# The low part of a weight tile: a negated copy on ACT and an adding DMA, instead of a subtraction on POOL

## The chip, the core and the metric

The program runs on one core of a Trainium2 chip. The metric is the time of one execution on the device in microseconds (us), as the median of several runs. The engines are TensorE (PE in the profile, its weight loads PEld), VectorE (DVE), ScalarE (ACT), GpSimd (POOL) and SyncE (SP, which here only issues DMAs).

## What is computed

Two layers of a decoder trunk over 512 tokens of width 1024, all in float32. Each layer projects the normalised input to the queries, keys and values of two kinds of attention and to gates; the results are merged, projected, normalised and added to the input; then comes a feed-forward block with a squared ReLU. Cut to the products, which are what the weights are loaded for:

```python
for layer in range(2):
    proj = rms_norm(x, g[0]) @ w_in            # 1024 -> 4504: q, k, v of both attentions, gates
    kc, vc = compress(k_c, w1[0]), compress(v_c, w1[1])   # blocks of 32 keys, MLP 2048 -> 256 -> 64
    y_nsa = sparse_attention(q, kc, vc, k_s, v_s, k_w, v_w, gates) @ w_nsa_o
    y_sb = stick_breaking_attention(sb_q, sb_k, sb_v) @ w_sb_o
    mixed = (sigmoid(g_a) * y_nsa + sigmoid(g_b) * y_sb) @ w_out
    x = x + rms_norm(mixed, g[1])
    ff = square(relu(rms_norm(x, g[2]) @ w_ff1)) @ w_ff2  # 1024 -> 4096 -> 1024
    x = x + rms_norm(ff, g[3])
```

## The kernel before

TensorE multiplies in a rounded float32 format (F32R). To keep float32's accuracy every operand is split in two: a high part, the value rounded, and a low part, the value minus the high part. A product of a weight w and an activation a is three matmuls into one bank of PSUM: w.hi x a.hi, w.hi x a.lo and w.lo x a.hi (`three`, L168 to L172).

Weights come in tiles of 128 x 1024 (512 KB), each with the weights of one output tile: 8 blocks of 128 x 128, so 24 matmuls over 512 tokens. A tile of the compression's `w1` feeds only 8 matmuls over 256 columns. `Weight` makes a tile ready in three steps, each on another engine. SP's queue loads it into `w_raw`, of which there are two buffers. ACT copies it, rounded, into `w_hi` (L146). POOL subtracts, raw minus high, into `w_lo` (L147). Three buffers each of `w_hi` and `w_lo` go round: a tile's copy can start when TensorE has finished with the tile three before. A few tiles of the compression have `sub=V`: there VectorE subtracts. Tiles whose tag isn't "w" (the first of a product after a norm) are made in two halves, on the same engines (L153, L154).

The order of TensorE's instructions is that of the program, written out by hand with a table of numbers (`PLAN`) that says how many matmuls of a projection stand between two steps of the attention. The orders of the other engines and of the DMA queues are made by a scheduler as the program is built. Every engine takes its instructions in order: what waits holds up all behind it.

A layer has these stages in the trace (layer 0, then layer 1 some 810 us later): the projections beside the sparse attention (to about 330 us, its first half up to about 165 us with the compression and the rotary embedding on VectorE), the merge and `w_out`, the norm and residual in `tail` (about 430 to 490 us), the feed-forward (to about 780 us), and another `tail`.

Of the kernel before, what the change touches and what calls it, by code (L numbers as in the profile page):

```python
# [8 lines left out]
F32 = mybir.dt.float32  # L9
F32R = mybir.dt.float32r  # L10
I32 = mybir.dt.int32
AF = mybir.ActivationFunctionType
ALU = mybir.AluOpType
# [12 lines left out]
P = 128  # L26
# [23 lines left out]
def layer_kernel(ctx, tc, xT, pos, gvec, tri, consts, smalls, w_in, w1, w_o, w_out, ff1, ff2, out):  # L50
    nc = tc.nc
    V, S, G, E = nc.vector, nc.scalar, nc.gpsimd, nc.tensor

    cp = ctx.enter_context(tc.tile_pool(name="cp", bufs=1))
    sp = ctx.enter_context(tc.tile_pool(name="sp", bufs=1))
# [6 lines left out]
    def big(tag, name, dt=F32):  # L62
        return sp.tile([P, T], dt, tag=tag, bufs=BUFS[tag], name=name)
# [4 lines left out]
    def psum(tag, name):  # L68
        return pp.tile([P, T], F32, tag=tag, bufs=2, name=name)
# [64 lines left out]
    class Weight:  # L134
        def __init__(self, src, tag="w", sub=None, between=None):
            raw = sp.tile([P, 1024], F32, tag="wr", bufs=2, name="w_raw")
            if between is None:
                nc.sync.dma_start(raw, src)
            else:
                nc.sync.dma_start(raw[:, 0:512], src[:, 0:512])  # L140
                between()
                nc.sync.dma_start(raw[:, 512:], src[:, 512:])
            if tag == "w":
                h = sp.tile([P, 1024], F32R, tag="wh", bufs=3, name="w_hi")
                l = sp.tile([P, 1024], F32R, tag="wl", bufs=3, name="w_lo")
                S.activation(h, raw, AF.Copy)  # L146
                (sub or G).tensor_tensor(l, raw, h.bitcast(F32), ALU.subtract)  # L147
                self.h, self.l = [h[:, 0:512], h[:, 512:]], [l[:, 0:512], l[:, 512:]]
            else:
                self.h = [big(tag, "w_hi", F32R) for _ in range(2)]  # L150
                self.l = [big(tag, "w_lo", F32R) for _ in range(2)]
                for j in range(2):
                    S.activation(self.h[j], raw[:, 512 * j:512 * j + 512], AF.Copy)  # L153
                    (sub or G).tensor_tensor(self.l[j], raw[:, 512 * j:512 * j + 512], self.h[j].bitcast(F32), ALU.subtract)  # L154
# [13 lines left out]
    def three(ps, w, k, act, first, last):  # L168
        ah, al = act
        E.matmul(ps, w.hi(k), ah, start=first, stop=False)  # L170
        E.matmul(ps, w.hi(k), al, start=False, stop=False)  # L171
        return E.matmul(ps, w.lo(k), ah, start=False, stop=last)  # L172
# [52 lines left out]
        return [(big("act", f"ah{k}", F32R), big("act", f"al{k}", F32R)) for k in range(KT)]  # L225

    def tail(l, n, mixed, acc, load, acts, prev, src, nxt, head):
        """The last output tiles of a product, its post-norm, the residual and the next pre-norm with the first tiles of
        the product that follows, in two halves of the tokens."""
        group = range(KT - GN, KT)  # L230
        last_sq = []
        na = new_acts() if nxt is not None else None
# [172 lines left out]
            return vc  # L405

    class Filler:
        """Products emitted one at a time between the steps of the attention; `late` holds what follows a product by some
        steps."""

        def __init__(self):
            self.gens, self.late, self.n = [], [], 0
# [27 lines left out]
                    self.late.pop(0)[1]()  # L440

    class Head:
        """The first four units of a product, their weights prepared ahead of it."""

        def __init__(self, src):
            self.src, self.ws = src, []
# [10 lines left out]
    def layer(l, acts, R, heads):  # L457
# [174 lines left out]
        groups = [(g, qt, b) for g in range(2) for qt in QORD[g] for b in range(2)]  # L632
        items, first, last, late_c = [], [], [], []
# [44 lines left out]
        score = [0, 0]  # L678

        def score_ahead(i, budget):  # L680
            """Scores of the groups whose items come soon after item i, a few heads at a time."""
            while score[0] < len(groups):
                j, h = score
                if first[j] > i + 1:
                    held = sum(need(k) for k in range(j) if last[k] > i)
                    if budget <= 0 or first[j] > i + PLAN["AH"] or held + need(j) > BUFS["P"]:
                        return
                nsa_scores(j, h)
                budget -= 1
                score[:] = [j, h + 1] if h < 3 else [j + 1, 0]  # L690
# [86 lines left out]
        def turn(i):  # L777
            j, kt = items[i]
            if kt == "c":
                fill.until(lambda: groups[j][0] in softmaxed)  # L780
            nsa_turn(items[i])
            score_ahead(i, PLAN["BU"])
# [29 lines left out]
        for h in range(4):  # L812
            score_ahead(0, 1)
            fill.run(PLAN["F2"])
# [84 lines left out]
        early = {}  # L899

        def mix_in(m, j, tag, last):
            """The first terms of output tile m's product with the attention j's output."""
            if m not in early:
                early[m] = Weight(w_o[l, m]), {}
            wo, banks = early[m]
            ps = psum(tag, "y")
            src = (o_nsa, o_sb)[j]
            banks[j] = ps, last
            for k in range(last):
                three(ps, wo, 4 * j + k, src[k], k == 0, k == 3)  # L910
                yield
# [87 lines left out]
        last = l + 1 == DEPTH  # L999
# [101 lines left out]
```

## Time and profile before

| | |
|---|---|
| median of 3 runs | 1643.62 us (1638.53 to 1645.77) |
| the profiled execution, from its first to its last instruction | 1643.4 us |
| TensorE (PE) busy | 1542.5 us, 94% |
| VectorE (DVE) busy | 911.0 us, 55% |
| POOL busy | 797.8 us, 49% |
| ACT busy | 725.5 us, 44% |
| DMA: share of 16 engines' time, on SP's queue | 27.1% |
| mean granted clock of TensorE | 0.972 |

The shares are means over the stages named above, in which different engines are busy. A busy TensorE isn't TensorE at its peak, since its matmuls are pipelined: in the feed-forward one 128x512 matmul begins every 0.23 us and is recorded as 0.389 us long.

### The profile page before, as it was taken

How to read it: one execution, taken by the hardware profiler on the slowest of the kernel's cores; microseconds unless marked ns; L12 is line 12 of the kernel's file. 1: busy time of each engine (PE TensorE's matmuls, PEld its weight loads, DVE VectorE, ACT ScalarE, POOL GpSimd, SP SyncE). 2: the span in 40 equal slices, each digit the busy share in tenths (PEclk: the TensorE clock that was granted, in tenths of full speed). 3: DMA queues.
4: the chain of work that ended last, by engine and by line, in shares of the span. 5: the costliest groups of instructions: out<-in, count | busy, mean ns of one | idle time of the engine just before them, and what ended most of it. 6: DMA issues, size and time to landing. Idle time of an engine off the chain costs nothing.

```text
span 1643.4 us, 20414 instructions
## 1 busy us (share of the span) xinstructions
PE 1542.5 (94%) x7706; PEld 1291.3 (79%) x7706; DVE 911.0 (55%) x1536; ACT 725.5 (44%) x1343; POOL 797.8 (49%) x519
## 2 busy tenths in 40 slices
PE   7688999999989999999987989999998999999996
PEld 5576778888878888887885767788878888888886
DVE  8998964355493232314599888533536823223246
ACT  6355764553453232324344567655433523233242
POOL 3674444435544444445557734444455344444443
PEclk9889999999999999999998999999999999999998
DMA  5221112223423233333322210122244132332321
GB/s 180 77 79 63 29 50 77 65 82 114 138 65 103 90 103 92 101 95 110 123 78 77 90 39 26 53 77 77 90 128 128 40 102 93 100 99 94 102 91 64
DMA packets 46002, 143.14 MB, mean 87 GB/s; under 512 B 5008, under 2 KB 11536, under 8 KB 45904
## 3 DMA queue, kind: packets, MB, share of 16 engines
q1 hardware_dynamic: 45680, 141.55, 27.1%
q8 instruction: 60, 0.98, 0.3%
q14 instruction: 38, 0.31, 0.1%
q0 software_dynamic: 80, 0.26, 0.0%
q10 hardware_dynamic: 144, 0.03, 0.0%
HBM read 137.11 MB, written 4.72 MB: 86 GB/s over the span
## 4 chain that ended last, share of the span: by engine, by line
PE 74%; DVE 19%; ACT 3%; issue 2%; DMA 1%; POOL 1%; SPq 0%; DVEq 0%; ACTq 0%; POOLq 0%
PE ff L170 12%; PE ff L171 12%; PE ff L172 12%; PE proj L469 5%; PE proj L467 5%; PE proj L465 5%; DVE pn L276 2%; DVE P L675 2%; PE y L171 2%; PE p_t L705 2%; PE y L170 2%; PE y L172 2%; PE tail L171 1%; PE tail L170 1%; PE tail L172 1%
## 5 line engine op out<-in xcount | busy, mean ns | idle before, releaser
L147 POOL TENSOR_TENSOR w_lo<-w_raw,w_hi 128x1024 fp32r<-128x1024 f32 x226 | 550.9, 2439 | 569.4 <-ACT w_hi L146 558.2
L146 ACT ACTIVATE w_hi<-w_raw 128x1024 fp32r<-128x1024 f32 x230 | 243.4, 1059 | 564.2 <-PE ff L171 391.1
L467 PE MATMUL proj<-al,w_hi 128*128 128x512 f32 x496 | 199.6, 402 | 0.0
L469 PE MATMUL proj<-ah,w_lo 128*128 128x512 f32 x496 | 199.6, 402 | 0.0
L465 PE MATMUL proj<-ah,w_hi 128*128 128x512 f32 x496 | 198.5, 400 | 0.0
L171 PE MATMUL ff<-hl,w_hi 128*128 128x512 f32 x448 | 174.4, 389 | 1.2 <-DVE hl L166 1.2
L170 PE MATMUL ff<-ah,w_hi 128*128 128x512 f32 x448 | 174.3, 389 | 0.0
L171 PE MATMUL ff<-al,w_hi 128*128 128x512 f32 x448 | 174.3, 389 | 0.0
L170 PE MATMUL ff<-hh,w_hi 128*128 128x512 f32 x448 | 174.3, 389 | 0.0
L172 PE MATMUL ff<-hh,w_lo 128*128 128x512 f32 x448 | 174.3, 389 | 0.0
L172 PE MATMUL ff<-ah,w_lo 128*128 128x512 f32 x448 | 174.3, 389 | 0.0
L166 DVE TENSOR_TENSOR hl<-relu,hh 128x512 fp32r<-128x512 f32 x64 | 108.2, 1696 | 80.1 <-ACT hh L165 79.9
L996 DVE TENSOR_TENSOR ffa<-ff,ffa 128x512 f32<-128x512 f32 x40 | 27.6, 691 | 155.9 <-PE ff L172 155.9
L467 PEld LDWEIGHTS proj<-al,w_hi 128*128 128x128 f32 x496 | 95.8, 193 | 17.2
L465 PEld LDWEIGHTS proj<-ah,w_hi 128*128 128x128 f32 x496 | 95.5, 193 | 17.0
L469 PEld LDWEIGHTS proj<-ah,w_lo 128*128 128x128 f32 x496 | 95.3, 192 | 17.1 <-POOL w_lo L147 0.3
L171 PEld LDWEIGHTS ff<-hl,w_hi 128*128 128x128 f32 x448 | 84.1, 188 | 19.1 <-DVE hl L166 1.6
L172 PEld LDWEIGHTS ff<-ah,w_lo 128*128 128x128 f32 x448 | 84.1, 188 | 17.6
L172 PEld LDWEIGHTS ff<-hh,w_lo 128*128 128x128 f32 x448 | 84.1, 188 | 17.6
L171 PEld LDWEIGHTS ff<-al,w_hi 128*128 128x128 f32 x448 | 84.1, 188 | 17.5
L170 PEld LDWEIGHTS ff<-hh,w_hi 128*128 128x128 f32 x448 | 84.1, 188 | 17.3
L170 PEld LDWEIGHTS ff<-ah,w_hi 128*128 128x128 f32 x448 | 84.1, 188 | 17.2
(308 smaller groups left out, 3353.6 us busy)
## 6 DMA issues: line engine op xcount, KB each, us to landing
w_raw<-in_ff_dram SPq DMA_DIRECT2D x128, 512.0 KB, 3.5
w_raw<-in_w_in_dram SPq DMA_DIRECT2D x69, 512.0 KB, 3.5
w_raw<-in_w_dram SPq DMA_DIRECT2D x16, 512.0 KB, 3.5
w_raw<-in_w_o_dram SPq DMA_DIRECT2D x16, 512.0 KB, 3.4
w_raw<-in_w_out_dram SPq DMA_DIRECT2D x16, 512.0 KB, 3.5
x<-in_xT_dram SPq DMA_DIRECT2D x8, 256.0 KB, 6.8
x_old<-in_xT_dram SPq DMA_DIRECT2D x8, 256.0 KB, 2.7
xsave<-x SPq DMA_DIRECT2D x8, 256.0 KB, 2.0
```

The costliest lines, as they stand in the source:

```text
L146: S.activation(h, raw, AF.Copy)
L147: (sub or G).tensor_tensor(l, raw, h.bitcast(F32), ALU.subtract)
L166: V.tensor_tensor(lo, src, hi.bitcast(F32), ALU.subtract)
L170: E.matmul(ps, w.hi(k), ah, start=first, stop=False)
L171: E.matmul(ps, w.hi(k), al, start=False, stop=False)
L172: return E.matmul(ps, w.lo(k), ah, start=False, stop=last)
L276: V.scalar_tensor_tensor(t, mixed[k][:, c], gcol(l, n, k), R[:, c], ALU.mult, ALU.mult)
L465: E.matmul(ps, w.hi(k), ah, start=(k == 0), stop=False)
L467: E.matmul(ps, w.hi(k), al, start=False, stop=False)
L469: E.matmul(ps, w.lo(k), ah, start=False, stop=(k == KT - 1))
L675: V.tensor_scalar(pr[h], pr[h], sm4[:, h:h + 1], None, ALU.mult)
L705: E.transpose(pt[:, P * h:P * h + P], pend[j][0][h][:, P * kt:P * kt + P], ident)
```

## The change

For a tile with tag "w" and no `sub`, POOL's subtraction goes away. ACT writes a second copy of the raw tile, with the factor -1 and rounded as the first, into `w_lo`: minus the high part. Then a DMA, issued by POOL, reads the tile again from memory and adds it to what stands in `w_lo`: the weight minus its high part, as before. So a second read of 512 KB a tile comes, and the high part is no longer an operand of the low part's making. `w_hi` and `w_lo` have four buffers instead of three; the room for them comes from the space in which descriptors of POOL's DMAs are kept, 4,096 bytes a partition instead of the usual. Tiles with another tag, and those with `sub`, are as they were. The diff also empties some comments, so that lines behind L147 move down by 4.

```diff
             if tag == "w":
-                h = sp.tile([P, 1024], F32R, tag="wh", bufs=3, name="w_hi")
-                l = sp.tile([P, 1024], F32R, tag="wl", bufs=3, name="w_lo")
+                h = sp.tile([P, 1024], F32R, tag="wh", bufs=4, name="w_hi")
+                l = sp.tile([P, 1024], F32R, tag="wl", bufs=4, name="w_lo")
                 S.activation(h, raw, AF.Copy)
-                (sub or G).tensor_tensor(l, raw, h.bitcast(F32), ALU.subtract)
+                if sub is None:
+                    S.activation(l, raw, AF.Copy, scale=-1.0)
+                    nc.gpsimd.dma_start(l, src, accum_op=ALU.add)
+                else:
+                    sub.tensor_tensor(l, raw, h.bitcast(F32), ALU.subtract)
...
-    nc = bacc.Bacc("TRN2", target_bir_lowering=False, num_devices=1)
+    nc = bacc.Bacc("TRN2", target_bir_lowering=False, num_devices=1, dynamic_dma_scratch_size=4096)
```

The scheduler's orders change with it. The first place is ACT at the start, where the first weights of tag "w" are made beside the first norm (`R_104`, from `ss`, the sum of squares) and the tables of the rotary embedding (`nround`, `s_342`, from `ang`). Before:

```order
L146 ACTIVATE w_hi<-w_raw 128x1024
L202 ACT_TABLE_LOAD
L202 ACTIVATE R_104<-ss,eps_c 128x256
L146 ACTIVATE w_hi<-w_raw 128x1024
L202 ACTIVATE R_104<-ss,eps_c 128x256
L204 ACT_TABLE_LOAD
L204 ACTIVATE R_104<-R_104 128x256 x2
L116 ACT_TABLE_LOAD
L116 ACTIVATE nround<-ang 128x512
```

And now:

```order
L146 ACTIVATE w_hi<-w_raw 128x1024
L148 ACTIVATE w_lo<-w_raw 128x1024
L146 ACTIVATE w_hi<-w_raw 128x1024
L148 ACTIVATE w_lo<-w_raw 128x1024
L206 ACT_TABLE_LOAD
L206 ACTIVATE R_104<-ss,eps_c 128x256 x2
L116 ACT_TABLE_LOAD
L116 ACTIVATE nround<-ang 128x512
L117 ACTIVATE s_343<-ang 128x512
L129 ACT_TABLE_LOAD
L208 ACTIVATE R_104<-R_104 128x256 x2
```

The third and the fourth tile of tag "w" now stand ahead of the norm's logarithm, the first of them was between its two halves; and the norm's exponential (L204 before, L208 now) has moved behind the sines.

The second place is POOL in the sparse attention of layer 0, where it scales probabilities (`P`) between weights of `w_in` and of the compression (`w`). Before:

```order
L673 TENSOR_TENSOR P<-P,sm_624 128x512 x2
L147 TENSOR_TENSOR w_lo<-w_raw,w_hi 128x1024 x2
L132 TENSOR_TENSOR sb0l<-sbf,sb0h 128x512
L673 TENSOR_TENSOR P<-P,sm_732 128x512 x2
L147 TENSOR_TENSOR w_lo<-w_raw,w_hi 128x1024 x2
```

And now:

```order
L677 TENSOR_TENSOR P<-P,sm_629 128x512 x2
L149 DMA w_lo<-in_w_in_dram 128x1024
L149 DMA w_lo<-in_w_dram 128x1024
L677 TENSOR_TENSOR P<-P,sm_740 128x512 x2
L132 TENSOR_TENSOR sb0l<-sbf,sb0h 128x512
L149 DMA w_lo<-in_w_dram 128x1024
L149 DMA w_lo<-in_w_in_dram 128x1024
```

The DMAs' issues stand where the subtractions stood, and the second scaling has moved ahead of `sb0l`.

## Rows read from the trace of the kernel before

**Rows 1.** The page's first part, without the weight loads: busy time, share of the span and number of instructions of each engine.

```profile
PE 1542.5 (94%) x7706; PEld 1291.3 (79%) x7706; DVE 911.0 (55%) x1536; ACT 725.5 (44%) x1343; POOL 797.8 (49%) x519
```

**Rows 2.** The page's chain of the work that ended last, by engine (shares of the span).

```profile
PE 74%; DVE 19%; ACT 3%; issue 2%; DMA 1%; POOL 1%; SPq 0%; DVEq 0%; ACTq 0%; POOLq 0%
```

**Rows 3.** Busy time of each engine in four stretches, in us, with the number of its instructions; then the granted clock of TensorE (1.00 is 2.4 GHz), the busy share of the DMA engines and what they moved.

```profile
20.00:165.00 145.00, 116.85 (x565) 92.78 (x563) 133.58 (x248) 77.01 (x162) 87.24 (x57) 0.89 0.25 77
...
410.00:493.00 83.00, 75.05 (x497) 69.54 (x496) 55.43 (x90) 40.73 (x80) 43.95 (x31) 0.96 0.32 102
493.00:739.00 246.00, 246.00 (x1087) 203.71 (x1086) 72.42 (x70) 74.22 (x92) 108.11 (x45) 1.00 0.31 97
...
862.00:987.00 125.00, 103.98 (x531) 83.99 (x531) 114.34 (x248) 69.96 (x165) 76.12 (x53) 0.90 0.21 68
```

**Rows 4.** The page's costliest groups, the two that make a tile's parts: operation, operands, count, then busy us and mean ns of one, then the engine's idle time before them and what ended it.

```profile
L147 POOL TENSOR_TENSOR w_lo<-w_raw,w_hi 128x1024 fp32r<-128x1024 f32 x226 | 550.9, 2439 | 569.4 <-ACT w_hi L146 558.2
L146 ACT ACTIVATE w_hi<-w_raw 128x1024 fp32r<-128x1024 f32 x230 | 243.4, 1059 | 564.2 <-PE ff L171 391.1
```

**Rows 5.** The timeline of layer 0 around 94 us, rows of POOL, VectorE and TensorE: start and duration in us (x2 are two instructions in a row), and in brackets the idle time before and who ended it.

```profile
94.58 5.13 POOL L147 TENSOR_TENSOR w_lo<-w_raw,w_hi 128x1024 fp32r<-128x1024 f32 x2
...
94.70 2.79 DVE L336 TENSOR_TENSOR xr<-qr,xr 64x512 fp32r<-64x512 f32 x1
...
96.99 0.33 PE L365 MATMUL cmp_h<-w_lo,bhl 128*64 128x256 f32 x1 [0.62 <-POOL w_lo L147]
...
98.14 1.66 DVE L382 TENSOR_TENSOR cmp_u<-cmp_u,cmp_ht 128x64 f32<-128x64 f32 x1
99.83 0.69 DVE L336 TENSOR_TENSOR xr<-qr,xr 64x512 fp32r<-64x512 f32 x1
```

**Rows 6.** Groups of VectorE's instructions from 20 to 165 us, shapes kept apart; the number before the last bar is the mean duration of one in ns.

```profile
L336 DVE TENSOR_TENSOR xr<-qr,xr 64x512 fp32r<-64x512 f32 x8 | 7.8, 972 | 1.1 <-ACT xr L335 0.8
L330 DVE TENSOR_TENSOR qr<-qr,rope_sh 128x512 f32<-128x512 f32 x3 | 7.1, 2383 | 0.0
...
L114 DVE SCALAR_TENSOR_TENSOR ang<-nround,ang 128x512 f32<-128x512 f32 x6 | 6.2, 1027 | 0.1
...
L522 DVE TENSOR_TENSOR K2w<-kr,K1w 64x512 fp32r<-64x512 f32 x2 | 4.2, 2105 | 0.0
...
L329 DVE TENSOR_TENSOR rope_sh<-rope_sh,sinT 128x512 f32<-128x512 f32 x4 | 3.8, 960 | 0.0
```

**Rows 7.** The same lines over the whole span, least, median and longest duration in ns.

```profile
L336 DVE TENSOR_TENSOR xr<-qr,xr x16: 684/688/2831, 65.3 to 908.7; 64x512 fp32r<-64x512 f32 x16
...
L330 DVE TENSOR_TENSOR qr<-qr,rope_sh x6: 670/2197/2901, 59.5 to 890.3; 128x512 f32<-128x512 f32 x6
...
L114 DVE SCALAR_TENSOR_TENSOR ang<-nround,ang x6: 676/682/2753, 26.5 to 36.5; 128x512 f32<-128x512 f32 x6
...
L522 DVE TENSOR_TENSOR K2w<-kr,K1w x4: 687/1186/2527, 68.9 to 881.4; 64x512 fp32r<-64x512 f32 x4
...
L329 DVE TENSOR_TENSOR rope_sh<-rope_sh,sinT x8: 669/712/1752, 52.0 to 887.7; 128x512 f32<-128x512 f32 x8
```

**Rows 8.** The groups of VectorE's instructions, as in group 6, from 862 to 987 us (layer 1).

```profile
L336 DVE TENSOR_TENSOR xr<-qr,xr 64x512 fp32r<-64x512 f32 x8 | 11.7, 1465 | 0.2
...
L330 DVE TENSOR_TENSOR qr<-qr,rope_sh 128x512 f32<-128x512 f32 x3 | 5.1, 1706 | 0.0
L329 DVE TENSOR_TENSOR rope_sh<-rope_sh,sinT 128x512 f32<-128x512 f32 x4 | 4.5, 1121 | 0.0
```

**Rows 9.** Busy time in two stretches of the instructions that write or read w_lo alone, columns as in group 3 without ACT.

```profile
20.00:165.00 145.00, 43.63 (x114) 21.62 (x113) 3.41 (x2) 42.88 (x18) 0.89 0.25 77
...
862.00:987.00 125.00, 35.50 (x93) 17.72 (x93) 3.39 (x2) 35.23 (x14) 0.90 0.21 68
```

**Rows 10.** Two rows of ACT's timeline in the feed-forward (start and duration in us): the copies of two tiles that follow each other.

```profile
565.27 1.06 ACT L146 ACTIVATE w_hi<-w_raw 128x1024 fp32r<-128x1024 f32 x1 [3.19 <-PE ff L171]
...
570.71 1.06 ACT L146 ACTIVATE w_hi<-w_raw 128x1024 fp32r<-128x1024 f32 x1 [3.19 <-PE ff L171]
```

**Rows 11.** The timeline at the start, rows of ACT and one of VectorE: start and duration in us.

```profile
26.26 1.04 ACT L146 ACTIVATE w_hi<-w_raw 128x1024 fp32r<-128x1024 f32 x1
27.32 1.28 ACT L202 ACT_TABLE_LOAD   x1
28.61 0.47 ACT L202 ACTIVATE R<-ss,eps_c 128x256 f32<-128x256 f32 x1
...
38.93 0.69 DVE L501 TENSOR_TENSOR kk<-head,R 128x512 f32<-128x512 f32 x1
```

**Rows 12.** DMA issues: first the one that POOL issues, in its timeline (start, duration of the issue), then the views of issues by line, with count, KB each and median us from issue to landing.

```profile
11.75 0.70 POOL L105 DMA_DIRECT2D pos_i<-in_pos_dram  x1
...
w_raw<-in_ff_dram SPq DMA_DIRECT2D x128, 512.0 KB, 3.5
...
pos_i<-in_pos_dram POOLq DMA_DIRECT2D x1, 256.0 KB, 6.1
```

## The prediction, made before the changed kernel was run

> **What bounds the kernel now.** I read the shares of the page first [rows 1]: TensorE is busy 94% of the span, POOL 49%, ACT 44%. A half-busy POOL proves nothing either way, so the chain that ended last comes next [rows 2]: TensorE 74%, VectorE 19%, POOL only 1%. The work that the change takes away is hardly ever the last thing waited for. The stretches say where [rows 3]: from 493 to 739 us (feed-forward) TensorE is busy without a gap, and its clock is granted at 1.00 (2.4 GHz). From 20 to 165 us and from 862 to 987 us (first half of the attention, one stretch a layer) VectorE is busy 133.6 of 145 us and 114.3 of 125 us, TensorE far less, with 0.89 and 0.90 of the clock. So there are two regimes: feed-forward, where preparing weights must only keep up, and the attention's start, where VectorE is late.
>
> **What the removed subtraction costs today.** There are 226 of them, 2,439 ns each, 550.9 us of POOL [rows 4]. In the feed-forward none is on the path. At the attention's start they are, through VectorE: the reader should lay the rows at 94 us side by side [rows 5]. POOL starts two subtractions at 94.58; VectorE's xr, begun at 94.70, takes 2.79 us, and the next xr, at 99.83, 0.69 us. In between, a 128x64 product takes 1.66 us, until POOL's second subtraction is done. A VectorE instruction with two operands in SBUF waits for the POOL subtraction to end.
>
> **Term 1, VectorE's waits.** The five costliest kinds of such instructions in layer 0 [rows 6], against the least that the same line ever took [rows 7]: xr 8 x (972 - 684) ns, qr 3 x (2,383 - 670), ang 6 x (1,027 - 676), K2w 2 x (2,105 - 687), rope_sh 4 x (960 - 669): 13.6 us. Layer 1 [rows 8], the same way: xr 6.2, qr 3.1, rope_sh 1.8: 11.2 us. So 24.7 us are seen in a few lines. The lower bound is 0 (other POOL operations cause some, and stay). The upper is the time in which the subtractions hold POOL in these stretches, 42.9 and 35.2, together 78 us [rows 9]. Many smaller lines, and VectorE's part of the norms (410 to 493 us, VectorE 55 of 83 us [rows 3]), wait as well, so I take 45 us of waiting removed, and of it two thirds, 30 us, as span: where VectorE stops being late, TensorE and ACT are next. **-30 us.** In the feed-forward the same waits vanish for nothing.
>
> **Term 2, ACT.** Each of the 226 tiles gets a second ACT pass over 128x1024; the first takes 1,059 ns [rows 4], so about +239 us, to 965 us of the span. In the feed-forward it is hidden: a product lasts 5.44 us (570.71 - 565.27 [rows 10]), and ACT works 74.2 of 246 us [rows 3], 1.6 us of each product. In the VectorE-bound stretches it is 32 tiles at most [rows 9], 34 us on an engine with over 50 us idle in each [rows 3]; the softmax exponentials queue behind it. ACT has 3% of the chain [rows 2]; I charge one part in seven, 5 us. **+5 us** (bounds 0 and 34).
>
> **Term 3, the start.** The order of ACT changes: with four buffers, four pairs of weight copies stand ahead of the first norm's logarithm, where there were two copies; and the norm's exponential now stands behind the rotary sine. Before, the second copy is at 26.26, a table load of 1.28 us follows, the logarithm begins at 28.61, and kk = head x R, the first thing VectorE does with the norm, at 38.93 [rows 11]. Now the fourth pair needs one of the two raw buffers, free when the second pair is done, 26.26 + 2.1 = 28.4; its load lands 3.5 us later [rows 12]; with its pair at 34.0, and a table load, the logarithm comes at 35.3, some 6.7 us later. VectorE has other work in between (the angles, which get shorter), so I charge **+4 us** (bounds 0 and 7).
>
> **Term 4, the wait that is added.** The low part is ready when a DMA has landed, not when POOL ends. The trace has one DMA from POOL's queue, half as large and without an addition: 0.70 us on POOL, 6.1 us from issue to landing; a plain load of a tile from SP lands in 3.5 us [rows 12]. No row shows an accumulating one. I take 6.1 us; the bounds are 3.5 and, twice the POOL row for twice the bytes, 12.2. In the feed-forward a fourth buffer lets a tile start three products, 16.3 us, before its use: 2 x 1.06 + 0.70 + 6.1 = 8.9 us fit, and even 12.2 does. The compression's weights have less room: a w1 tile feeds only 8 short products, and TensorE already waited 0.62 us for one at 96.99 [rows 5]. Issued where that subtraction began, its low part would land at 94.58 + 0.70 + 6.1 = 101.4, 4.4 us later than TensorE needs it; the fourth buffer gives part back. What queues behind it on TensorE are the transposes that VectorE and ACT wait for. I charge 2 us a layer, **+4 us** (bounds 0 and 18, at 4.4 us for two tiles of each layer).
>
> POOL itself gets lighter (0.70 instead of 2.44 us a tile); its remaining operations come earlier, and I book nothing for that.
>
> **The sum.** 1643.4 - 30 + 5 + 4 + 4 = 1626 us, against the profiled execution's own span of 1643.4 us; the median of the runs is 1643.62, so nothing has to be shifted. 0.5%, 8.2 us, is about what a measurement of this kernel can tell from no change: faster is under 1635.4, slower over 1651.8.
>
> **Rivals.** *The DMA engines become the bound* (slower). In the feed-forward they are busy 0.31 of the time [rows 3], 1.69 us of every 5.44 for one plain load a tile. The accumulation shares the same engines and comes once a tile too: 3.75 us are free for it, 2.2 plain loads. From there on every product waits. If reading the source, reading the destination and writing each cost a plain load, it is 5.07 us: 6.76 instead of 5.44 a tile, 1.32 more. Of the 226 tiles I count 165 as bound by TensorE (all but the 32 of [rows 9] and some 30 at the norms): +218 us, 1844 us. With 4.2 us it is +0.45 a tile, 1700 us. For it: no row shows an addition in a DMA. Against it: a plain load leaves 69% of the engines free. The Trainium skill, "Collectives: The Full Stack", The bandwidth ceiling, says that a reducing transfer runs at half the rate of a copy, since it makes two reads on the same ring, and that the addition itself costs nothing. By it the accumulation would be an estimated 3.38 us, 5.07 of 5.44 us in all: the engines would just keep up, and the sum would stay at 1626; no row here shows it. I give this rival 0.25, half of it above 1790 us.
>
> *The gain is eaten* (same): the waits on landing at the compression and the later start cost their upper bounds, 7 + 18 us, and the gain is 30: 1643 + 5 - 5 = 1643 us. For it: TensorE's order is fixed, so each late tile stops everything behind it. Chance 0.15.
>
> *The waits move up* (slower, mildly): landing is near 12.2 us instead of 6.1, the fourth buffer gives back a third of the difference, and each of the 12 w1 tiles that aren't subtracted on VectorE comes 4 us later still: 1626 + 48 = 1674 us. Chance 0.10.
>
> *The forecast*, between 1590 and 1635: 0.48; beyond it, because nearly all 78 us come back: 0.02.
>
> **The numbers.** Faster 0.48 + 0.02 = 0.50, same 0.15, slower 0.25 + 0.10 = 0.35. The likeliest case alone spans 1590 to 1635. The range must reach into the slower cases: 1590 to 1790 leaves out 0.02 below and some 0.13 above.
>
> **What the profile after would show.** Term 1: xr, qr and K2w near their least, VectorE under 120 us of busy time in 20 to 165 us. Term 2: a second ACT group of 226 at about 1,060 ns. Term 3: kk at about 43 us. Term 4: waits of TensorE on a DMA into w_lo, small, at cmp_h and not at ff. The DMA share in the feed-forward tells the rival: under 0.9, and products 5.44 us apart, and it is refuted; near 1.0 with ff waiting for w_lo, and the forecast falls. It is also wrong if VectorE's lines do not shorten although POOL is free.

## The result and the profile after

The changed kernel takes 1665.07 us (median of four runs, 1663.85 to 1667.40) against 1643.73 of the kernel before beside it: 1.0139 times as long, 95% interval 1.0122 to 1.0157. It is slower; I had forecast 1626 us and faster. The profiled execution has a span of 1663.3 us, 19.9 more than before.

First the shares of the page, then the chain of the work that ended last, by engine ([rows 1, 2]), and ACT's two passes and one kind of POOL's issues ([rows 4]; mean ns of one, then the idle time before them):

```profile
PE 1545.7 (93%) x7706; PEld 1291.6 (78%) x7706; DVE 738.8 (44%) x1536; ACT 930.1 (56%) x1568; POOL 439.9 (26%) x519
...
PE 71%; DVE 11%; DMA 9%; ACT 5%; issue 3%; POOL 0%; SPq 0%; ACTq 0%; DVEq 0%; POOLq 0%
...
L146 ACT ACTIVATE w_hi<-w_raw 128x1024 fp32r<-128x1024 f32 x230 | 243.4, 1059 | 436.6 <-PE ff L175 272.0
L149 POOL DMA_DIRECT2D w_lo<-in_ff_dram x120 | 105.4, 878 | 542.6 <-ACT w_lo L148 501.4
L148 ACT ACTIVATE w_lo<-w_raw 128x1024 fp32r<-128x1024 f32 x226 | 235.6, 1042 | 0.2
```

VectorE loses 172 us of busy time and falls from 19% of the chain to 11%: the first term did happen. But the DMA engines rise from 1% to 9%, and ACT from 3% to 5%. The stretches ([rows 3], same columns) show it from the engines' side: VectorE 111.12 instead of 133.58 us in the first, TensorE 68.09 instead of 75.05 in the second, no change of TensorE in the third.

```profile
20.00:165.00 145.00, 117.54 (x572) 93.47 (x570) 111.12 (x251) 93.28 (x181) 62.56 (x59) 0.89 0.61 145
410.00:493.00 83.00, 68.09 (x433) 61.39 (x432) 39.98 (x71) 40.89 (x74) 29.36 (x31) 0.92 0.67 170
493.00:739.00 246.00, 246.00 (x1112) 204.79 (x1112) 55.74 (x89) 119.86 (x146) 38.62 (x44) 1.00 0.85 186
```

Who TensorE waits for now (us in all, times, longest) names the tiles. The feed-forward's steady products (ff) do not wait for a landing, and wait once for ACT; the last tiles of a product (tail) and the first tiles of the next (head) do wait for landings:

```profile
PE tail L176 <- DMA w_lo<-in_w_out_dram: 10.1, 2, 6.2
PE head L176 <- DMA w_lo<-in_w_in_dram: 8.2, 1, 8.2
...
PE tail L176 <- DMA w_lo<-in_ff_dram: 5.1, 1, 5.1
...
PE proj L473 <- DMA w_lo<-in_w_in_dram: 4.6, 2, 2.3
PE ff L174 <- ACT hh L169: 3.8, 1, 3.8
```

And the chain ahead of such a tail tile, piece by piece (start, us, what):

```profile
409.42 7.61 DMA w_raw<-in_w_out_dram
...
418.10 1.05 ACT w_lo L148
...
419.16 8.03 DMA w_raw<-in_w_out_dram
...
431.24 0.95 ACT w_lo L148
...
432.21 9.11 DMA w_raw<-in_w_out_dram
...
444.64 6.82 DMA w_lo<-in_w_out_dram
...
451.50 0.58 PE tail L176
```

Only the last piece is the landing that I had priced. The other DMA pieces are plain loads of the raw tile, 7.6 to 9.1 us long where the kernel before took 3.5 [rows 12], and two of them start in the instant in which ACT's second pass ends, which frees the raw buffer and lets POOL start the accumulation. The DMA queues (share of 16 engines' span) and issues (median us to landing) of the whole span:

```profile
q0 software_dynamic: 32624, 118.77, 40.7%
q1 hardware_dynamic: 45680, 141.55, 27.8%
...
w_raw<-in_ff_dram SPq DMA_DIRECT2D x128, 512.0 KB, 5.8
w_lo<-in_ff_dram POOLq DMA_DIRECT2D x120, 512.0 KB, 7.7
...
w_raw<-in_w_out_dram SPq DMA_DIRECT2D x16, 512.0 KB, 5.0
w_lo<-in_w_out_dram POOLq DMA_DIRECT2D x14, 512.0 KB, 8.0
```

From here on "landing" is from a DMA's issue until its data are there.

### The profile page after: what moved, and what is told of

It reads as the page before. It is cut to its first block, busy times and chain, and to the rows that moved or that the text cites. A ratio compares the mean times of both kernels' runs of the same rounds, so it can differ in the third digit from the quotient of the medians.

```text
span 1663.3 us, 20886 instructions
## 1 busy us (share of the span) xinstructions
PE 1545.7 (93%) x7706; PEld 1291.6 (78%) x7706; DVE 738.8 (44%) x1536; ACT 930.1 (56%) x1568; POOL 439.9 (26%) x519
## 4 chain that ended last, share of the span: by engine, by line
PE 71%; DVE 11%; DMA 9%; ACT 5%; issue 3%; POOL 0%; SPq 0%; ACTq 0%; DVEq 0%; POOLq 0%
PE ff L175 12%; PE ff L176 12%; PE ff L174 12%; PE proj L471 6%; PE proj L473 6%; PE proj L469 6%; DMA w_raw<-in_w_out_dram 2%; DMA w_raw<-in_w_in_dram 2%; DVE pn L280 2%; PE p_t L709 2%; ACT w_lo L148 2%; DMA w_raw<-in_ff_dram 2%; DVE P L679 1%; PE tail L176 1%; PE y L176 1%
## 5 line engine op out<-in xcount | busy, mean ns | idle before, releaser
L149 POOL DMA_DIRECT2D w_lo<-in_ff_dram x120 | 105.4, 878 | 542.6 <-ACT w_lo L148 501.4
L148 ACT ACTIVATE w_lo<-w_raw 128x1024 fp32r<-128x1024 f32 x226 | 235.6, 1042 | 0.2
L469 PE MATMUL proj<-ah,w_hi 128*128 128x512 f32 x496 | 199.1, 401 | 0.0
L149 POOL DMA_DIRECT2D w_lo<-in_w_in_dram x64 | 56.8, 888 | 190.6 <-ACT w_lo L148 170.4
L170 DVE TENSOR_TENSOR hl<-relu,hh 128x512 fp32r<-128x512 f32 x64 | 44.9, 704 | 136.4 <-ACT hh L169 136.4
L175 PEld LDWEIGHTS ff<-hl,w_hi 128*128 128x128 f32 x448 | 84.4, 188 | 18.6 <-DVE hl L170 1.1
```

Of the source, the lines that this page charges most:

```text
L148: S.activation(l, raw, AF.Copy, scale=-1.0)
L149: nc.gpsimd.dma_start(l, src, accum_op=ALU.add)
L170: V.tensor_tensor(lo, src, hi.bitcast(F32), ALU.subtract)
L469: E.matmul(ps, w.hi(k), ah, start=(k == 0), stop=False)
```

## The experiments

The kernel before was run again beside each group of experiments, with medians from 1640.2 to 1643.7 us: differences between kernels of different groups are good to some 4 us.

Lengths of the stretches of one profiled execution, in us, each from the start of TensorE's first instruction of a kind to that of the next (ng, z, wout, ff, the second tail, the next layer's ng or the end); layer 0 / layer 1:

| kernel | start | ng to z | z to wout | wout to ff | ff to tail | tail to ng / end |
|---|---|---|---|---|---|---|
| before | 37.4 | 199.1 / 193.2 | 171.2 / 171.2 | 81.3 / 82.5 | 306.2 / 304.7 | 57.0 / 39.6 |
| after | 46.0 | 194.4 / 191.3 | 169.3 / 170.2 | 90.3 / 86.7 | 311.2 / 304.7 | 60.0 / 39.1 |
| no low part (e4) | 34.0 | 179.8 / 174.4 | 169.3 / 169.3 | 77.4 / 77.4 | 306.0 / 304.7 | 54.6 / 39.1 |
| no addition (e3) | 36.2 | 195.0 / 190.0 | 169.3 / 169.3 | 74.0 / 74.9 | 306.3 / 304.7 | 51.9 / 39.1 |
| plain copy (e2) | 38.9 | 196.6 / 190.1 | 169.3 / 169.3 | 74.7 / 74.9 | 308.4 / 304.7 | 52.4 / 39.1 |
| bursts by POOL (e9) | 36.4 | 194.4 / 191.2 | 169.3 / 171.0 | 76.2 / 74.8 | 312.1 / 304.7 | 52.6 / 39.4 |
| addend from SBUF (e18) | 41.8 | 195.6 / 191.0 | 170.9 / 170.9 | 82.7 / 80.3 | 307.5 / 304.7 | 59.7 / 39.1 |
| early release (e16) | 44.2 | 189.1 / 184.8 | 171.0 / 169.4 | 87.4 / 89.5 | 309.3 / 304.7 | 55.7 / 39.1 |
| late release (e17) | 45.9 | 193.5 / 194.5 | 170.3 / 173.8 | 84.0 / 86.8 | 311.7 / 304.7 | 59.3 / 45.4 |
| both remedies (e14) | 37.7 | 186.2 / 181.7 | 170.9 / 169.3 | 76.6 / 75.8 | 313.9 / 304.7 | 54.7 / 39.1 |

Against before, the change wins 9.5 us in the attention (the second and third columns) and loses 30 at the start, between wout and ff, and from ff to the next ng in layer 0. Most of the 5 us from ff to the tail there is the one wait of 3.8 us for hh, the hidden units of the feed-forward, near its end: the next layer's first tiles are loaded among its own there, ACT waits for raw loads, and the hidden units stand behind them in its order. Two theories for the loss. **Bursts**: where tiles are made in quick succession, the landing and the raw loads beside it stand on the path. **Something that was put in besides**: the fourth buffer, the second ACT pass, or the order of instructions that a scheduler makes anew for each kernel.

**Four runs take the change apart.**

> The kernel before with the fourth buffer (and the smaller scratch for it) and nothing else of the change: POOL still subtracts. Theory (the 21 us are lost where weight tiles are remade in a burst, at the start and around w_out, tail and head, because the raw loads and the landing of the accumulation stand on the path): the fourth buffer costs nothing by itself, 1640 to 1647 us. Rival (the loss is the order that four buffers give ACT and SP, at the start above all): about 1650 us, with kk some 5 us later than before.

```
kernel before:  tag="wh", bufs=3  ->  bufs=4;   tag="wl", bufs=3  ->  bufs=4;   scratch 4096
```

1643.10 us, 1.0006 of before (0.9996 to 1.0015). The buffer alone does nothing, at the start neither.

> The changed kernel, with the accumulating DMA made a plain one of the same bytes, from the same queue, in the same order on every engine (the low part is then the whole weight: this part of the computation is changed). Theory: only the part of the loss that is the addition in the DMA goes, which is a shorter landing (some 5 instead of 7.7 us) and less traffic beside the raw loads (3.5 to 4 instead of 5 to 6 us each): 1650 to 1657 us. Rival 1 (the second ACT pass and the new order are the loss): unchanged, 1662 to 1668. Rival 2 (the traffic of the addition is all of it): back to 1640 to 1645.

```diff
-                    nc.gpsimd.dma_start(l, src, accum_op=ALU.add)
+                    nc.gpsimd.dma_start(l, src)
```

1620.25 us, 0.9881 (0.9853 to 0.9909), below all three ranges. It has the order of the changed kernel on every engine, so the difference to 1665.07, 44.8 us (42 by the two ratios), is the addition in the DMA and nothing else. By the table it lies in the bursts: 7.1 us at the start, 27.4 between wout and ff, 10.4 from there to the next ng, and nothing in the attention. Its queue and landings, to be laid beside those above:

```profile
q0 software_dynamic: 32624, 118.77, 20.9%
...
w_raw<-in_ff_dram SPq DMA_DIRECT2D x128, 512.0 KB, 3.7
w_lo<-in_ff_dram POOLq DMA_DIRECT2D x120, 512.0 KB, 4.7
...
w_raw<-in_w_out_dram SPq DMA_DIRECT2D x16, 512.0 KB, 3.6
```

The same bytes hold the engines 0.209 x 1618.2 / 226 = 1.50 us a tile; with the addition it is 0.407 x 1663.3 / 226 = 3.00 us, twice as long. The raw loads are back at 3.7 us, although the plain copy reads memory too and starts at the same moment as the accumulation did, 0.27 us behind a raw load (start and duration in us; SP's duration spans several loads in a row):

```profile
568.55 16.65 SPq L138 DMA_DIRECT2D w_raw<-in_ff_dram  x4
...
568.82 0.53 POOL L149 DMA_DIRECT2D w_lo<-in_ff_dram  x1 [4.91 <-ACT w_lo L148]
```

> The changed kernel without the DMA that adds the weight: ACT still writes two passes over a tile, the low part is the weight times 2 to the minus 12 (this part of the computation is changed). No landing, no traffic, no subtraction on POOL. Theory: the losses around w_out, tail and head (18 us) go with the landing and the slow raw loads, the two layers' gain of about 10 us in the attention stays, and the start keeps part of its loss: 1632 to 1643 us. Rival 1 (the second ACT pass holds the raw buffers and is the loss): 1655 to 1665.

```diff
-                    S.activation(l, raw, AF.Copy, scale=-1.0)
-                    nc.gpsimd.dma_start(l, src, accum_op=ALU.add)
+                    S.activation(l, raw, AF.Copy, scale=2.0 ** -12)
```

1611.25 us, 0.9812 (0.9796 to 0.9829), below both ranges: a plain transfer with its landing costs only 9.0 us.

> The changed kernel without any work for the low part: its products use the high part twice (this part of the computation is left out), so ACT makes one pass, POOL subtracts only the tiles of other tags, no second DMA. What POOL's 226 subtractions cost the kernel before in all. My prediction's first term says 30 us: 1610 to 1620 us. If the gain was mis-sized and is the 10 us that the stretches of the changed kernel's attention show: 1628 to 1636.

```diff
-                    S.activation(l, raw, AF.Copy, scale=-1.0)
-                    nc.gpsimd.dma_start(l, src, accum_op=ALU.add)
+                    l = h
```

1588.01 us, 0.9676 (0.9662 to 0.9691), below both ranges too. POOL's 226 subtractions cost 1641.6 - 1588.0 = 53.6 us, more than my 30; from ng to z alone it is 19 us in each layer. And the second ACT pass costs 1611.2 - 1588.0 = 23.2 us, 15 of it in each layer's attention (195.0 - 179.8, 190.0 - 174.4), less what comes back later. The first stretch, 20 to 165 us, of e4 and then of e3: TensorE does 129.39 and 123.89 us of work in it, 116.85 before.

```profile
20.00:165.00 145.00, 129.39 (x684) 105.21 (x683) 125.33 (x324) 94.76 (x212) 49.43 (x48) 0.95 0.27 84
```

```profile
20.00:165.00 145.00, 123.89 (x630) 99.71 (x629) 116.53 (x290) 102.70 (x205) 46.49 (x43) 0.92 0.26 84
```

So 1641.6 - 53.6 + 23.2 + 9.0 + 44.8 = 1665.0 us. The sum closes by construction, since each term is the difference of two whole kernels; all but the last contain what the scheduler made of the edit.

**Where and how the addition costs.**

> The changed kernel with all its work for the low part (second ACT pass, accumulating DMA), but TensorE reads the high part in its place (this part of the computation is left out), so nothing waits for the landing. The addition costs 45 us (1665 against 1620 with a plain transfer). Theory A (the loss is mainly the raw loads, which land after 5.8 instead of 3.6 us beside the accumulation, with two raw buffers only): the loss stays, 1645 to 1660 us. Theory B (the loss is the wait for the landing, 7.7 instead of 4.7 us): it goes, 1611 to 1625 us. Near the middle, 1635: both carry it.

```diff
-                self.h, self.l = [h[:, 0:512], h[:, 512:]], [l[:, 0:512], l[:, 512:]]
+                self.h = self.l = [h[:, 0:512], h[:, 512:]]
```

1887.07 us, 1.149 (1.145 to 1.154): outside both, since the edit did something else too. As nothing reads the low part, ACT's order changed: in the feed-forward, the second pass of one tile stands ahead of the first pass of the tile before. One of the two raw buffers is held meanwhile, and loads run one at a time. ACT's second pass idles 695.3 us (0.2 in the changed kernel), and DMA has 46% of the chain:

```profile
DMA 46%; ACT 20%; PE 19%; DVE 9%; issue 5%; POOL 1%; ACTq 0%; SPq 0%; DVEq 0%; POOLq 0%
...
L148 ACT ACTIVATE w_lo<-w_raw 128x1024 fp32r<-128x1024 f32 x226 | 238.8, 1057 | 695.3 <-DMA w_raw<-in_ff_dram 465.8
```

It doesn't decide between A and B, but shows that with TensorE waiting for no landing of a low part the raw buffers' cycle can cost over 200 us more than the change did.

> The changed kernel with three raw buffers instead of two, nothing else edited. Theory A (raw loads): a load can start a tile earlier, and most of the loss around w_out, tail and head goes: 1635 to 1650 us. Theory B (landing): little, 1655 to 1665 us, since the accumulation starts only a little earlier.

```diff
-            raw = sp.tile([P, 1024], F32, tag="wr", bufs=2, name="w_raw")
+            raw = sp.tile([P, 1024], F32, tag="wr", bufs=3, name="w_raw")
```

1651.65 us, 1.0061 (1.0037 to 1.0085), 13 under the changed kernel: part of the loss, between the two ranges and nearer to theory A's. The scheduler made another order here too.

> The changed kernel, with POOL's subtraction back for the tiles that are wanted in quick succession alone: the heads' fourth tiles, the output weights between the merge and the tail, the tails (some 22 of 226 tiles). The other 204 keep the accumulating DMA, the 112 of the feed-forward's steady part among them. If the addition's 45 us are lost in these bursts: 1625 to 1638 us. If the steady traffic costs them: 1650 to 1665 us.

```diff
-        def load(self, sub=None, between=None):
+        def load(self, sub=G, between=None):
...
-                dense(ps, Weight(w_out[l, m]), merged)
+                dense(ps, Weight(w_out[l, m], sub=G), merged)
```

The two tails' weights get sub=G in the same way.

1625.81 us, 0.9924 (0.9900 to 0.9948): faster than both kernels. It is 24 tiles, not 22 as I had counted. Taking them back wins 39 us; the 202 others, 112 of them in the feed-forward, leave the time 5.6 us over the plain copy. The stretch 493 to 739 us shows that traffic without harm, the DMA engines 0.89 busy and TensorE without a gap, although the feed-forward's raw loads land in 5.3 us here as well:

```profile
493.00:739.00 246.00, 246.00 (x1087) 203.82 (x1087) 46.16 (x67) 115.79 (x134) 39.44 (x45) 1.00 0.89 193
```

> The kernel without any low part (1588 us), plus one accumulating DMA of the same 512 KB a tile from POOL's queue, from the high part into four SBUF tiles that nothing reads (part of the computation is left out as there, and the few subtractions on VectorE too). It has the traffic, no second ACT pass and no wait of TensorE for a landing. If the traffic beside the raw loads carries the addition's cost: 1610 to 1630 us. If the wait for the landing does: 1585 to 1598 us.

On the kernel without a low part, with four tiles `idle` that are zeroed once:

```diff
+    idle = [cp.tile([P, 1024], F32, name=f"idle{i}") for i in range(4)]
...
                     l = h
+                    idle_tile = idle[next(turn) % 4]; nc.gpsimd.dma_start(idle_tile, h.bitcast(F32), accum_op=ALU.add)
```

1598.46 us, 0.9745 (0.9720 to 0.9771): 10.5 over e4 and half a microsecond over the second range. The raw loads were hardly slowed, which I had not expected of either:

```profile
idle<-w_hi POOLq DMA_DIRECT2D x226, 512.0 KB, 6.2
w_raw<-in_ff_dram SPq DMA_DIRECT2D x128, 512.0 KB, 3.9
```

So an accumulation does not slow every load beside it: this one starts at the same moment as in the changed kernel, 0.27 us behind a raw load in the median, but takes its addend from SBUF. The next runs move the moment at which a raw buffer comes free, and with it the next load. In the changed kernel SP starts a load 0.27 us ahead of POOL's accumulation (columns as for the plain copy):

```profile
588.03 1.04 ACT L148 ACTIVATE w_lo<-w_raw 128x1024 fp32r<-128x1024 f32 x1
589.10 16.65 SPq L138 DMA_DIRECT2D w_raw<-in_ff_dram  x4
589.37 0.88 POOL L149 DMA_DIRECT2D w_lo<-in_ff_dram  x1 [4.56 <-ACT w_lo L148]
```

> The changed kernel, with ACT's second pass reading the high part instead of the raw tile (minus the rounded weight either way), so that a raw buffer is free 1.06 us earlier in each cycle of load and passes. If the cycle of the two raw buffers carries the loss in the bursts: 1650 to 1660 us. If the landing does: 1663 to 1667 us.

```diff
-                    S.activation(l, raw, AF.Copy, scale=-1.0)
+                    S.activation(l, h.bitcast(F32), AF.Copy, scale=-1.0)
```

1641.41 us, 1.0002 (0.9985 to 1.0018): 24 us won with a buffer that is free 1.06 us earlier, below both ranges. The load now starts well ahead of the accumulation, 1.74 us in these rows, and in the feed-forward both are short again:

```profile
591.83 11.21 SPq L138 DMA_DIRECT2D w_raw<-in_ff_dram  x3
592.23 1.04 ACT L148 ACTIVATE w_lo<-w_hi 128x1024 fp32r<-128x1024 f32 x1
593.57 0.87 POOL L149 DMA_DIRECT2D w_lo<-in_ff_dram  x1 [4.56 <-ACT w_lo L148]
...
w_raw<-in_ff_dram SPq DMA_DIRECT2D x128, 512.0 KB, 3.7
w_lo<-in_ff_dram POOLq DMA_DIRECT2D x120, 512.0 KB, 5.8
```

But the scheduler had changed the order again, so the 24 us need not be the moment's alone. A first control did not test it:

> The run before (second pass from the high part, 1641 us) with one added ACT instruction of a single column that reads the raw tile behind the second pass, so the raw buffer comes free at the moment the accumulation starts, as in the changed kernel. If the two transfers starting together are the cause: raw loads in the feed-forward land after over 5 us again (3.7 in the run before), the accumulation after over 7 (5.8), and the time is 1655 to 1672 us. If the order of the other instructions brought the gain: 1640 to 1650 us and landings as in the run before. The added instruction itself is 226 times some 0.2 us on ACT, of which a sixth on the path at most, 8 us.

It took 1667.98 us, 1.018 (1.015 to 1.021), inside the first range, but the raw loads landed in 4.3 us and the accumulations in 6.6, under what that needs: the added instruction, S.activation(held, raw[:, 0:1], AF.Copy), read the raw tile alone and mostly stood ahead of the second pass, in the feed-forward even ahead of the first, where ACT waits for the raw load and the hidden units come late (TensorE waits 14.2 us for them, 3.9 in e12). It shows nothing on the moment of release, but that an added instruction and a new order alone can cost 27 us (1667.98 against 1641.41). Two runs have the instruction bound to its place by its operands:

> The second pass from the high part (1641 us), plus one ACT instruction of a single column between the two passes, which reads the raw tile and the high part: the raw buffer is released some 0.2 us behind the first pass, about 1 us before the accumulation can start. What the added instruction costs by itself: 1641 to 1655 us, raw loads of the feed-forward landing after about 3.7 us and accumulations after about 5.8 us as without it.

> The same, with the added instruction behind the second pass, reading the raw tile and the low part, so that the raw buffer is released just when the accumulation may start. If the two transfers that start together collide: raw loads of the feed-forward over 5 us, accumulations over 7 us, and 10 to 25 us more than the run with the early release. If the gain of the second pass from the high part was another order of the instructions: equal to the run with the early release within 5 us, and the landings as there.

The early release (e16) and, below it, the late one (e17), against e12:

```diff
+                    S.activation(held, raw[:, 0:1], AF.Copy, scale=h[:, 0:1].bitcast(F32))
                     S.activation(l, h.bitcast(F32), AF.Copy, scale=-1.0)
...
                     S.activation(l, h.bitcast(F32), AF.Copy, scale=-1.0)
+                    S.activation(held, raw[:, 0:1], AF.Copy, scale=l[:, 0:1].bitcast(F32))
```

1645.00 us, 1.0024 (1.0012 to 1.0037), against 1672.38 us, 1.0185 (1.0150 to 1.0221): 27 us between the same instruction ahead of the second pass and behind it, 2 more than the first theory's upper bound. The landings of the early release, then of the late one:

```profile
w_raw<-in_ff_dram SPq DMA_DIRECT2D x128, 512.0 KB, 4.4
w_lo<-in_ff_dram POOLq DMA_DIRECT2D x120, 512.0 KB, 6.3
```

```profile
w_raw<-in_ff_dram SPq DMA_DIRECT2D x128, 512.0 KB, 5.3
w_lo<-in_ff_dram POOLq DMA_DIRECT2D x120, 512.0 KB, 7.7
```

The late release brings back nearly the landings of the changed kernel (5.8 and 7.7), and a loss of the same size. The loss goes with the landings: TensorE waits 57.5 us in all for landings in w_lo, 25.6 with the early release. But it lies elsewhere than the changed kernel's, 18 us in the attention and 10 in the tails (last columns of the table), while the bursts between wout and ff are 6 us shorter; and the scheduler's order differs between the two as well, on VectorE in 190 of 1,536 places. Last, whether the two must read the same memory:

> The changed kernel, whose accumulating DMA adds the high part, which is in SBUF, instead of the weight in memory, onto minus half of the weight (this part of the computation is changed). Same bytes, same moment (0.27 us behind the next raw load), and TensorE waits for the landing as in the changed kernel. If the collision is two transfers that read memory at once: raw loads of the feed-forward near 3.9 us and landings near 6.2 as in the run where nothing reads the sums, and 1625 to 1645 us. If any accumulation at this moment does it: raw loads over 5 us, landings over 7, 1655 to 1668 us.

```diff
-                    S.activation(l, raw, AF.Copy, scale=-1.0)
-                    nc.gpsimd.dma_start(l, src, accum_op=ALU.add)
+                    S.activation(l, raw, AF.Copy, scale=-0.5)
+                    nc.gpsimd.dma_start(l, h.bitcast(F32), accum_op=ALU.add)
```

1646.52 us, 1.0033 (1.0014 to 1.0053), 18.6 under the changed kernel and 1.5 over the first range, whose landings came as forecast:

```profile
w_lo<-w_hi POOLq DMA_DIRECT2D x226, 512.0 KB, 6.1
w_raw<-in_ff_dram SPq DMA_DIRECT2D x128, 512.0 KB, 3.9
```

This run too has the changed kernel's order on every engine, and its accumulation starts 0.27 us behind a raw load. So the 44.8 us of the addition have two parts. Some 18.6 go when the addend comes from SBUF: an accumulation that reads memory and a raw load that start together are both late. Neither half does that alone: a plain copy from memory at that moment leaves the load at 3.7 us (e2), an accumulation from SBUF at 3.9; and 1.74 us between the two (e12, median of the feed-forward) leave it at 3.7 as well. Whether it is the read of memory or the longer time on the DMA engines, 3.00 us a tile against 2.68, is not separated. The other 26.3 (1646.52 - 1620.25) are the slower addition itself, which lands after 6.1 us instead of 4.7 and holds the engines 0.369 x 1644.1 / 226 = 2.68 us instead of 1.50; half of them fall between wout and ff, where tiles are made in bursts (82.7 and 80.3 us, against 74.7 and 74.9 of the plain copy). Open stays how the 27 us between e16 and e17 divide between the slower transfers and the buffer that is free a microsecond later: no run holds one of them fixed.

**Better versions.**

> Accumulation only for the weights that feed TensorE during the attention (the products with the input weights and 12 tiles of the compression); the heads, the output weights and the feed-forward keep POOL's subtraction. The stretches say: the attention keeps its gain of 6.7 and 3.8 us, the start and the bursts are as before: 1632 to 1638 us. If the attention's gain depended on POOL being free elsewhere too: 1640 to 1645 us.

1634.66 us, 0.9947 (0.9925 to 0.9968), the time as expected (sub=G everywhere but in `product` and the compression), but not for the reason given: in its profiled execution the attention is only 1.4 and 2.4 us shorter than before, not 6.7 and 3.8; the rest of the gain is outside it.

> Accumulation only for every second tile of the products with the input weights, POOL's subtraction for all else. Without any low part the attention is 19 us shorter in each layer, with the second ACT pass alone only 4: so ACT takes most of the gain, and half of the tiles on each engine could beat either: 1625 to 1635 us. If the waits of VectorE for the remaining subtractions keep most of the loss: 1636 to 1643 us.

1640.80 us, 0.9995 (0.9981 to 1.0010; sub=None only for odd tiles of `product`): in the second range. That VectorE's remaining waits take the gain, as is said there, no run shows.

> The kernel with accumulation in the attention only (1635 us), but POOL writes minus the rounded weight (one operand in SBUF instead of two) in place of ACT's second pass. If VectorE waits only for a POOL instruction with two operands in SBUF, ACT's 15 us a layer come back: 1605 to 1622 us. If it waits for this one too: 1636 to 1650 us.

On e7:

```diff
-                    S.activation(l, raw, AF.Copy, scale=-1.0)
+                    G.tensor_scalar(l, h.bitcast(F32), -1.0, None, ALU.mult)
```

1646.87 us, 1.0038 (1.0026 to 1.0049): slower than e7. POOL needs 2,907 ns for it, more than for the subtraction that it replaces (2,423 in the same run), so the low part is later: in the attention TensorE waits 26.7 us for landings in w_lo, 6.0 in e7. VectorE hardly waits for the multiplication: its TENSOR_TENSOR instructions in the attention that begin during one (87) take 0.14 us longer in the mean than the shortest of the same instruction in any run; those that begin during a subtraction in the kernel before (77) take 0.83 us longer. So the time lies in the second range for another cause than the one stated there.

```profile
L148 POOL TENSOR_SCALAR w_lo<-w_hi 128x1024 fp32r<-128x1024 f32 x74 | 214.3, 2907 | 77.8 <-ACT w_hi L146 75.6
```

> Bursts by POOL (1626 us) and the second pass from the high part (1641 us) together. If both take away the same loss in the bursts: 1620 to 1628 us. If the earlier release also shortens the attention (7.2 and 6.0 us there): 1608 to 1618 us.

1613.59 us, 0.9844 (0.9825 to 0.9862): 3.1% under the changed kernel, 1.6% under the one before, and the best of the kernels here that compute the same. The attention is 186.2 and 181.7 us long (194.4 and 191.3 in the changed kernel), so the earlier release helps there too. What it still loses against before is layer 0's ff to tail, 313.9 us against 306.2: TensorE's one wait there for hh, behind ACT's waits for raw loads, is 5.1 us.

> The same with three raw buffers. If the cycle of load and passes is the limit still: 5 us or more under the run with two. If the two remedies left nothing of it: equal within 3 us.

1614.49 us, 0.9852 (0.9835 to 0.9869): equal: a third raw buffer wins nothing more in all.

## Why the prediction was wrong

**Term 1, VectorE's waits: right in kind, too small.** I took 30 of at most 78 us; without any low part it is 53.6, 38 of it from ng to z. The signs came: VectorE works 111.12 us in 20 to 165 us, under the 120 that I had asked for, and of the three kinds that I had named xr is at its least there, the two others two thirds of the way down to theirs ([rows 6], same columns):

```profile
L340 DVE TENSOR_TENSOR xr<-qr,xr 64x512 fp32r<-64x512 f32 x8 | 5.5, 686 | 0.3
...
L334 DVE TENSOR_TENSOR qr<-qr,rope_sh 128x512 f32<-128x512 f32 x3 | 3.6, 1191 | 0.0
...
L526 DVE TENSOR_TENSOR K2w<-kr,K1w 64x512 fp32r<-64x512 f32 x2 | 2.4, 1190 | 0.0
```

Both choices were too low, the 45 us of waiting and the two thirds of them: all 45 would still have been 8.6 short. Only the bound of 78 held.

**Term 2, the second ACT pass: mis-sized.** Each second pass takes 1,042 ns, near what I said, and the feed-forward hides it in its steady products. But the part on the path was 23.2 us, not 5. "One part in seven" came from ACT's 3% of the chain of before, where VectorE was the late one. Once VectorE was freed, ACT was next, as my own sentence on term 1 said ("TensorE and ACT are next") without a price.

**Term 3, the start: booked at half its size, and wrong in cause.** kk starts at 47.30 us instead of my 43, the first ng 8.6 us later than before, beyond my bound of 7. The order of ACT, which I blamed, is the same in e2, and costs 1.5 us there; the other 7.1 go with the addition. ACT's rows show the fourth pair waiting 5.09 us for a raw load that was issued at 27.46, just ahead of POOL's accumulations at 27.73 and 30.48; I had given that load 3.5 us, and it took 7.8:

```profile
29.15 1.04 ACT L148 ACTIVATE w_lo<-w_raw 128x1024 fp32r<-128x1024 f32 x1
35.28 1.06 ACT L146 ACTIVATE w_hi<-w_raw 128x1024 fp32r<-128x1024 f32 x1 [5.09 <-DMA w_raw<-in_w_in_dram]
```

**Term 4, the landing: the step that failed.** My 6.1 us for a landing was near (5.8 in e12, 7.7 in the changed kernel), and the steady products hid it as I said. (The 0.70 us that POOL needs to issue I counted twice: time to landing runs from the start of the issue.) Two things were left out. I asked whether a tile fits into a steady product and at the compression, and not around wout, tail and head, where 24 tiles are made in bursts; giving those back to POOL wins 39 us, and at the compression (cmp_h) TensorE waited 1.8 us in all. And I priced the new transfer by what waits for it, never by what it does to the transfer beside it: the raw load, started by the same event, went from 3.5 to 5.8 us in the median and to 9.1 at a tail. In place of +4, bounds 0 and 18, the runs showed +53.8: 9.0 for the plain transfer, 44.8 for the addition (7.1 of them at the start, in term 3's place).

**The rivals.** The DMA engines did not become the bound: busy 0.85 in the feed-forward, under my 0.9, and its length unchanged in layer 1 (304.7 us). The price of the estimate was nearly right: 3.00 us for 3.38, twice the engine time of a copy. The Trainium skill, "Collectives: The Full Stack", The bandwidth ceiling, says half the rate of a copy for a reducing transfer; by 3.00 against 1.50 us a tile the trace agrees. "The engines just keep up" was true as an average and no answer for the bursts. "The waits move up" (1674) came nearest in time, by another way: its landing of 12.2 us and its late w1 tiles didn't occur. The largest term of loss was in none of the rivals. That 1665 us lies between 1590 and 1790 is luck: the range reached that far for the DMA rival, which did not come.

## What to carry to other kernels

When work is moved to a DMA, look for what starts at the same moment: an event that both frees a load buffer and starts an accumulation from memory makes the two collide, where a plain copy at the same moment did no harm, and letting the buffer go a step earlier (here by reading the high part instead of the raw tile) staggers them without another instruction. Test a new latency where tiles are made in bursts, at the start and at the seams of stages, not in the steady loop; keep the old way for those few tiles. And where an engine is relieved, price the extra work on the next engine as if it stood on the path, not by its share of a chain that is about to change.

## What the runs showed of the hardware that I had not expected

An accumulating DMA of 512 KB from POOL's queue held the engines 3.00 us against 1.50 for a copy. A plain load and, 0.27 us behind it, an accumulation that reads memory took 5.8 and 7.7 us where 1.74 us apart (both medians of the feed-forward) they took 3.7 and 5.8; with the addend from SBUF, 0.27 us apart, it was 3.9 and 6.1, and with a plain copy from memory in the accumulation's place 3.7 and 4.7. POOL's multiplication of one operand by a constant (128x1024) took 2,907 ns, its subtraction of two 2,423 in the same run; VectorE's TENSOR_TENSOR instructions of the attention became 0.83 us longer in the mean during a subtraction (in the kernel before), 0.14 us during a multiplication.
